# RMSNorm of a matrix product: the order of the last row block's stores, and row block 4 stored in row halves

## The chip, the cores and the metric

One core of a Trainium2 chip. The metric is the device time of one execution in microseconds (us), the median of several. The time of an execution is a little longer than the span of its profile (220.8 against 219.0 us in the profiled run of before); the span runs from the first to the last instruction only.

## The reference

```python
def reference(a, b, gamma, eps):            # a, b: 2048 x 2048 fp32, gamma: 2048
    x = np.matmul(a, b)
    rms = np.sqrt(np.mean(x ** 2, axis=-1, keepdims=True) + eps)
    return (gamma * x / rms).astype(np.float32)
```

## The kernel before

The 2048 rows are 16 row blocks of 128. The product is computed in groups of two row blocks by seven half-size products in place of eight, in 16-bit floats; a group takes two halves `j`, each of which fills 512 columns in each half of the matrix's width. A row block's result sits in two fp32 tiles `x` of 128x1024; it is scaled in place by gamma and the inverse rms, and SyncE stores it. The tiles rotate through a few slots, so a later group writes where an earlier block was.

The store, and the hook that calls it during the following group:

```python
    def store(mb, order=(0, 1)):
        for h in order:
            nc.sync.dma_start(out=rows(mb, h * HALF, (h + 1) * HALF), in_=x_half.pop((mb, h)))
    # ... (hooks of the first half of a group; nxt = 2 * g + 2)
                hook(3, scale, 2 * g - 2)
                hook(4, apply, nxt + 1)
                hook(4, store, 2 * g - 2)
    # ... (hooks of the second half of a group)
            if g + 2 < NG:
                hook(0, load_after, g, nxt + 2)      # 1 MB of input, issued by GpSimd,
                # ...                                # once x_chunk(2 * g + 1, 1) is there
                    hook(0, load_block, nxt + 3)     # 1 MB more
```

The start of a half of a group. `x22` of the group that computes blocks 8 and 9 lies in the slot of block 4's second tile, so ScalarE's copy (L597, after the change L602) has to wait until that tile's store has landed:

```python
        x11, x12, x21, x22 = (x_chunk(ra, c1), x_chunk(ra, c2), x_chunk(rb, c1), x_chunk(rb, c2))
        # ...
        product(g, j, *one)
        nc.scalar.copy(out=c, in_=one[1])            # L597; c is x22
        last_squares()
        at_hook(1)
        product(g, j, *two)
        # ... six more products
```

The end of the last group (`rb` is row block 15, `xb` its left tile, `right` a tile with its right half):

```python
        r_b = inverse_rms(half_sq[:, 1:2], part)
        nc.vector.tensor_scalar_mul(out=xb[:, 0:CH], in0=xb[:, 0:CH], scalar1=r_b)
        nc.sync.dma_start(out=rows(rb, 0, CH), in_=xb[:, 0:CH])               # L809, 256 KB
        by_r(right[:, 0:CH], r_b)                                             # ScalarE
        for bank, col in zip(half, halves):
            scaled_gamma(right[:, CH:][:, col], bank, r_b, gam[3][:, col])    # VectorE
        nc.sync.dma_start(out=rows(rb, HALF, N), in_=right)                   # L813, 512 KB
        by_r(xb[:, CH:], r_b)                                                 # ScalarE
        nc.scalar.dma_start(out=rows(rb, CH, HALF), in_=xb[:, CH:])           # L815, 256 KB
```

Of the kernel before, what the change touches and what calls it, by code (L numbers as in the profile page):

```python
# [17 lines left out]
def kernel(  # L18
# [13 lines left out]
    nc = tc.nc  # L32
    P = 128
# [6 lines left out]
    CH = 512  # L40
    NCH = N // CH
    HALF = N // 2
    HB = 4
# [48 lines left out]
    for h, queue in enumerate((nc.sync, nc.scalar)):  # L92
        queue.dma_start(out=a0f[:, 2 * h:2 * h + 2, :],
                        in_=a[2 * h * P:(2 * h + 2) * P, 0:W2].rearrange("(r p) k -> p r k", p=P))
# [201 lines left out]
    x_half = {}  # L296
# [16 lines left out]
    def x_tile(mb, h):  # L313


        if (mb, h) not in x_half:
            n = n_x[0]
            n_x[0] += 1
            if n < 8:
                slot = n  # L320
            else:
                g = n // 4
                slot = ((0, 4, 1, 5), (0, 1, 4, 5))[g // 2 % 2 == 0][n % 4] + 2 * (g % 2)
            x_half[mb, h] = x_slot[slot]
        return x_half[mb, h]
# [29 lines left out]
    def inverse_rms(last, partial):  # L355
        return inverse(root(last, partial))

    def rows(mb, lo, hi):
        return out[mb * P:(mb + 1) * P, lo:hi]
# [12 lines left out]
                op0=ALU.mult, op1=ALU.mult)  # L372

    def store(mb, order=(0, 1)):
        for h in order:
            nc.sync.dma_start(out=rows(mb, h * HALF, (h + 1) * HALF), in_=x_half.pop((mb, h)))

    def finish(mb, order=(0, 1)):
        for h in order:
            scale(mb, (h,))  # L380
            store(mb, (h,))
# [252 lines left out]
    def hooks_of(g, j):  # L634
# [13 lines left out]
        if j == 0:  # L648
            if g == G0:
# [13 lines left out]
                hook(2, scale, 1, (0,))  # L663
                hook(4, apply, nxt + 1)
                hook(4, store, 1, (0,))
                hook(7, late.insert, 0, (r2, None))
            else:
# [13 lines left out]
                hook(3, row_factor, nxt + 1)  # L681
                hook(4, apply, nxt + 1)
                hook(4, store, 2 * g - 2)
        else:
            if g == G0:
# [19 lines left out]
    def last_group():  # L705
# [3 lines left out]
        ra, rb = 2 * g, 2 * g + 1  # L709
        x11, x12, x21, x22 = ([x_chunk(mb, 2 * j + c) for j in range(2)]  # L710
                              for mb in (ra, rb) for c in range(2))
        xa, xb = x_tile(ra, 0), x_tile(rb, 0)
# [24 lines left out]
        def by_r(x, r):  # L737
            nc.scalar.activation(out=x, in_=x, func=ACTF.Copy, scale=r)  # L738
# [68 lines left out]
        r_b = inverse_rms(half_sq[:, 1:2], part)  # L807
        nc.vector.tensor_scalar_mul(out=xb[:, 0:CH], in0=xb[:, 0:CH], scalar1=r_b)
        nc.sync.dma_start(out=rows(rb, 0, CH), in_=xb[:, 0:CH])  # L809
        by_r(right[:, 0:CH], r_b)  # L810
        for bank, col in zip(half, halves):
            scaled_gamma(right[:, CH:][:, col], bank, r_b, gam[3][:, col])
        nc.sync.dma_start(out=rows(rb, HALF, N), in_=right)  # L813
        by_r(xb[:, CH:], r_b)
        nc.scalar.dma_start(out=rows(rb, CH, HALF), in_=xb[:, CH:])  # L815

    for g in range(G0, NG - 1):
        for j in range(2):
            group_half(g, j, hooks_of(g, j))
    last_group()  # L820

# [33 lines left out]
```

## Time and profile before

| | before |
|---|---|
| median of 3 runs | 220.94 us (220.91 to 221.03) |
| span of the profile | 219.0 us |
| TensorE busy | 95% |
| last matmul's end to the end of the span | 7.0 us |
| last store's issue to its landing | 3.5 us |

The first four lines say that TensorE bounds the kernel up to its last matmul, and that 7 us follow in which it does nothing. A change that touches no matmul can gain only in those 7 us. It can lose anywhere, if it makes TensorE wait.

### The profile page before, as it was taken

Reading aid. Unit: us, or ns where it says so; the run is one execution under the profiler, and the core shown is the slowest. Engines: PE = TensorE matmul, PEld = TensorE weight load, DVE = VectorE, ACT = ScalarE, POOL = GpSimd, SP = SyncE. Lnnn points to the kernel's source line nnn. Section 1 sums busy time; section 2 is a strip of 40 time slices with the busy share of each in tenths; the row PEclk is TensorE's granted clock in tenths of the full one; section 3 lists DMA queues with packets and bytes.
Section 4 is the critical chain, followed back from the end, with each engine's and each line's share of the span. In section 5 each row is a group of like instructions: output and inputs, shape, how many; then the busy total and the mean of one; then the engine's idle time right before and its main releaser. Section 6 shows DMA issues by size and latency. Waiting matters only on the chain.

```text
span 219.0 us, 3023 instructions
## 1 busy us (share of the span) xinstructions
PE 208.8 (95%) x1012; PEld 98.4 (45%) x1032; DVE 165.9 (76%) x326; ACT 127.0 (58%) x263; POOL 36.2 (17%) x75
## 2 busy tenths in 40 slices
PE   7999999999999999999999999999999999999970
PEld 3544544444455444444444444444444444444440
DVE  1228799999899998988794649856794759787781
ACT  2110002920599898788646996289747996334471
POOL 7644433433020002100200002000200000000040
PEclk9999999999999999999999999999999999999996
DMA  7999999999939698939899049955799349145045
GB/s 152 175 202 206 204 206 209 210 208 224 414 91 332 232 278 214 379 153 263 213 294 381 19 87 272 355 233 96 174 291 396 57 89 365 69 178 208 1 179 206
DMA packets 36864, 46.60 MB, mean 213 GB/s; under 512 B 22256, under 2 KB 26352, under 8 KB 35568
## 3 DMA queue, kind: packets, MB, share of 16 engines
q0 software_dynamic: 10608, 23.86, 44.3%
q1 hardware_dynamic: 25824, 22.02, 33.4%
q10 hardware_dynamic: 416, 0.52, 0.7%
q8 instruction: 8, 0.13, 0.2%
q14 instruction: 8, 0.07, 0.1%
HBM read 34.60 MB, written 16.78 MB: 235 GB/s over the span
## 4 chain that ended last, share of the span: by engine, by line
PE 91%; DMA 3%; issue 1%; ACT 1%; POOL 1%; DVE 0%; ACTq 0%; POOLq 0%
PE acc L285 71%; PE acc L388 16%; DMA early<-in_a_dram 3%; PE tbank L419 2%; PE tbank L168 2%; PE acc L799 1%; POOL b L102 0%; PE tbank L185 0%; PE acc L185 0%; ACT x L738 0%; DVE head_at L173 0%; ACT sq L802 0%; ACT rms L352 0%; POOL t_left masks.py:199 0%; POOL t_left masks.py:197 0%
## 5 line engine op out<-in xcount | busy, mean ns | idle before, releaser
L285 PE MATMUL acc<-b,s 128*128 128x512 bf16 x397 | 92.7, 379 | 0.7
L285 PEld LDWEIGHTS <-s 128*128 128x128 f16 (+1 forms) x512 | 50.0, 98 | 59.6 <-DVE s L260 0.2
L388 PE MATMUL acc<-b,head_at 128*128 128x512 bf16 x171 | 42.2, 379 | 0.4 <-DMA b<-in_b_dram 0.3
L303 ACT ACTIVATE sq<-x 128x512 bf16<-128x512 f32 x53 | 33.4, 630 | 6.9 <-DVE x L731 3.0
L370 DVE SCALAR_TENSOR_TENSOR x<-x,r,gamma_sb 128x1024 f32<-128x1024 f32 x28 | 34.9, 1281 | 0.7
L219 ACT ACTIVATE sq<-a 128x1024 bf16<-128x1024 f32 x24 | 25.3, 1053 | 2.0 <-DMA a<-in_a_dram 1.4
L388 PEld LDWEIGHTS <-head_at 128*128 128x128 bf16 x176 | 16.9, 98 | 19.5 <-issue 0.7
L242 ACT ACTIVATE head_at<-a,s 128x2048 f16<-128x2048 f32 x10 | 20.0, 1998 | 3.4 <-DVE s L229 3.3
L102 POOL DMA_DIRECT2D b<-in_b_dram x32 | 17.2, 540 | 20.4 <-DMA b<-in_b_dram 14.1
L430 ACT COPY x<-acc 128x512 f32<-128x512 f32 x5 | 2.9, 582 | 24.6 <-PE acc L388 24.6
L285 PEld LDWEIGHTS <-head_at 128*128 128x128 f16 (+1 forms) x112 | 11.0, 98 | 13.2
L285 PEld LDWEIGHTS <-at_even 128*128 128x128 f16 x96 | 9.4, 98 | 11.3
L285 PE MATMUL acc<-early,head_at 128*128 128x512 bf16 x63 | 14.4, 379 | 0.1
L285 PE MATMUL acc<-early,s 128*128 128x512 bf16 x56 | 14.2, 379 | 0.0
L260 DVE TENSOR_TENSOR s<-head_at 128x1024 f16<-128x1024 f16 (+5 forms) x22 | 13.4, 636 | 0.1
L615 DVE TENSOR_TENSOR x<-x,x 128x512 f32<-128x512 f32 x9 | 6.2, 692 | 8.8 <-ACT x L613 8.3
L127 POOL COPY pace<-x 128x1 f32<-128x1 f32 x4 | 1.7, 413 | 66.3 <-DVE x L624 65.0
L597 ACT COPY x<-acc 128x512 f32<-128x512 f32 x9 | 5.2, 573 | 11.5 <-PE acc L285 7.7
L285 PE MATMUL acc<-t_left,s 128*128 128x512 bf16 x47 | 11.3, 379 | 0.1
L783 POOL TENSOR_SCALAR x<-x,r 128x512 f32<-128x512 f32 x1 | 2.7, 2653 | 51.2 <-DVE r L346 51.2
L276 DVE TENSOR_TENSOR b<-b 128x1024 bf16<-128x1024 bf16 x16 | 10.8, 686 | 0.2
L173 DVE COPY head_at<-tbank 128x1024 bf16<-128x1024 bf16 x7 | 4.8, 692 | 8.0 <-PE tbank L168 7.9
(113 smaller groups left out, 239.3 us busy)
## 6 DMA issues: line engine op xcount, KB each, us to landing
out_dram<-x SPq DMA_DIRECT2D x29, 512.0 KB, 3.7
a<-in_a_dram POOLq DMA_DIRECT2D x10, 1024.0 KB, 8.6
b<-in_b_dram POOLq DMA_DIRECT2D x32, 256.0 KB, 9.9
a<-in_a_dram POOLq DMA_DIRECT2D x4, 512.0 KB, 9.8
early<-in_a_dram POOLq DMA_DIRECT2D x7, 256.0 KB, 10.0
gamma_sb<-in_gamma_dram POOLq DMA_DIRECT2D x2, 512.0 KB, 8.3
out_dram<-x SPq DMA_DIRECT2D x3, 256.0 KB, 2.6
out_dram<-a SPq DMA_DIRECT2D x1, 512.0 KB, 3.3
```

Of the source, the lines that this page charges most:

```text
L102: nc.gpsimd.dma_start(out=raw[j][kp][:, t, :], in_=b[lo:lo + P, j * HALF:(j + 1) * HALF])
L173: nc.vector.tensor_copy(out=head_at[:, 2 * kp:2 * kp + 2, :, :], in_=view)
L219: nc.scalar.activation(out=junk, in_=a32[mb][:, h * HALF:(h + 1) * HALF], func=ACTF.Square, scale=2.0 ** -8, accum_out=n2[:, h:h + 1])
L242: nc.scalar.activation(out=a16[mb], in_=a32.pop(mb), func=ACTF.Copy, scale=factor.pop(mb))
L260: nc.vector.tensor_tensor(out=sum_of(g, s)[:, lo:hi, :], in0=x[:, lo:hi, :], in1=y[:, lo:hi, :], op=op)
L276: nc.vector.tensor_tensor(out=flat[:, 1:3, :], in0=flat[:, 1:3, :], in1=flat[:, 0::3, :], op=ALU.add)
L285: nc.tensor.matmul(bank, lhsT[:, kp, :], rhs, start=(start and kp == 0), stop=(kp == KP - 1), skip_group_check=not start)
L303: nc.scalar.activation(out=sq[:, 0:CH], in_=src, func=ACTF.Square, scale=inv_sqrt_n, accum_out=msq[mb][:, c:c + 1])
L370: nc.vector.scalar_tensor_tensor(out=x, in0=x, scalar=inverse_of[mb], in1=gamma_sb[:, h * HALF:(h + 1) * HALF], op0=ALU.mult, op1=ALU.mult)
L388: nc.tensor.matmul(bank, head_at[:, kt, r, :], head_rhs(c, kt), start=(kt == 0), stop=(kt == KT - 1))
L597: nc.scalar.copy(out=c, in_=one[1])
L615: nc.vector.tensor_tensor(out=t, in0=t, in1=x12, op=ALU.add)
```

## The change

The intent: the last 1 MB of output should go to memory without a hole, from one queue, and its last store should be the one behind which the fewest closing waits stand. ScalarE scales `xb`'s second chunk ahead of `right`'s first. Row block 4 is cut in row halves, two transfers more, by which the transfers' semaphores rotate two further.

```diff
     def store(mb, order=(0, 1)):
+        step = P // 2 if mb == HB else P
         for h in order:
-            nc.sync.dma_start(out=rows(mb, h * HALF, (h + 1) * HALF), in_=x_half.pop((mb, h)))
+            x = x_half.pop((mb, h))
+            for lo in range(0, P, step):
+                nc.sync.dma_start(
+                    out=out[mb * P + lo:mb * P + lo + step, h * HALF:(h + 1) * HALF],
+                    in_=x[lo:lo + step, :])
@@
         nc.sync.dma_start(out=rows(rb, 0, CH), in_=xb[:, 0:CH])
+        by_r(xb[:, CH:], r_b)
+        nc.sync.dma_start(out=rows(rb, CH, HALF), in_=xb[:, CH:])
         by_r(right[:, 0:CH], r_b)
         for bank, col in zip(half, halves):
             scaled_gamma(right[:, CH:][:, col], bank, r_b, gam[3][:, col])
         nc.sync.dma_start(out=rows(rb, HALF, N), in_=right)
-        by_r(xb[:, CH:], r_b)
-        nc.scalar.dma_start(out=rows(rb, CH, HALF), in_=xb[:, CH:])
```

All lines of the kernel after are five further down than those of before: L597 is L602, L376 (the store) is L379.

## The prediction

> **What bounds the kernel now.** I read the page first, then the chain of work that ended last in order of time, then the timeline, the DMA windows and SyncE's waits over the last six microseconds.
>
> ```profile
> span 219.0 us, 3023 instructions
> PE 208.8 (95%) x1012; PEld 98.4 (45%) x1032; DVE 165.9 (76%) x326; ACT 127.0 (58%) x263; POOL 36.2 (17%) x75
> ```
>
> TensorE is busy 95% of the span. The chain, read in order of time, leaves TensorE only at the very end:
>
> ```profile
> 210.21 1.76 PE acc L799 x16
> ...
> 212.05 0.48 ACT sq L802 x2
> ...
> 212.89 0.17 DVE r L346
> ...
> 213.08 0.03 ACT a L738
> 213.11 0.60 issue
> 213.71 0.70 ACT x L738
> ```
>
> Columns are start, duration, what. TensorE's last matmul ends at 211.97. The chain view stops at 214.41, with ScalarE's last scaling, yet the span lasts to 219.0. The missing 4.6 us are a store, its landing and the program's closing waits. Nothing in the change touches a matmul, so a gain can only come from the 219.0 - 211.97 = 7.0 us after the last one, and mostly from those 4.6. The timeline of that stretch (start, duration, engine, line, tile; SPq and ACTq are the sequencers that issue transfers):
>
> ```profile
> 213.08 0.72 ACT L738 ACTIVATE a<-a,r 128x512 f32<-128x512 f32 x1 [0.23 <-DVE r L346]
> 213.09 0.49 DVE L808 TENSOR_SCALAR x<-x,r 128x512 f32<-128x512 f32 x1
> 213.49 0.87 DVE L734 SCALAR_TENSOR_TENSOR a<-acc,r,gamma_sb 128x256 f32<-128x256 f32 x2
> 213.60 0.33 SPq L809 DMA_DIRECT2D out_dram<-x  x1
> 213.71 0.70 ACT L738 ACTIVATE x<-x,r 128x512 f32<-128x512 f32 x1
> 214.42 0.33 SPq L813 DMA_DIRECT2D out_dram<-a  x1
> 214.45 0.36 ACTq L815 DMA_DIRECT2D out_dram<-x  x1
> ```
>
> The reader is to see that the first 256 KB store (L809) leaves at 213.60, and the remaining 768 KB only at 214.42 and 214.45, together. In between, a finished chunk (`right`, done on ScalarE at 213.80) waits for its other half. The windows below show what the 16 DMA engines do (the last two columns are their busy share and GB/s):
>
> ```profile
> 214.50:214.75 0.25, 0.00 (x0) 0.00 (x0) 0.00 (x0) 0.00 (x0) 0.00 (x0) 1.00 0.99 377
> 214.75:215.00 0.25, 0.00 (x0) 0.00 (x0) 0.00 (x0) 0.00 (x0) 0.00 (x0) 0.84 1.01 385
> 215.00:215.25 0.25, 0.00 (x0) 0.00 (x0) 0.00 (x0) 0.00 (x0) 0.00 (x0) 0.50 0.66 205
> ...
> 217.00:217.25 0.25, 0.00 (x0) 0.00 (x0) 0.00 (x0) 0.00 (x0) 0.00 (x0) 0.50 0.89 320
> 217.25:217.50 0.25, 0.00 (x0) 0.00 (x0) 0.00 (x0) 0.00 (x0) 0.00 (x0) 0.50 0.16 49
> ```
>
> They are full from 214.45, sag to 0.66 around 215.2, are full again, and stop at about 217.4. The sag is the hole between L809's packets and those of the two late stores; in the trace's packets it is about 0.17 us per engine (L809's end near 215.15, the next start near 215.3). The end then is:
>
> ```profile
> L850 SPq EVENT_SEMAPHORE  x4: 28/28/28, 217.9 to 218.1; - x4
> L850 SPq DRAIN  x2: 7/7/7, 218.2 to 218.2; - x2
> ```
>
> These are SyncE's instructions of the closing line between 217.7 and 218.3. The last transfer, L815 on ScalarE's queue, lands 3.5 us after its issue (landing column of its line), at 217.90. Only then do four waits follow at 217.92, 217.98, 218.04 and 218.10, one each 0.06 us, then two drains at 218.17 and 218.23, and 0.8 us of barrier to 219.0. SyncE goes through its transfer semaphores in a fixed order, two to an instruction.
>
> [...] both queues are in flight from 215.7 to 217.3 and the rate stays at 352 to 434 GB/s, as with one queue alone (377 and 385 above). [...] L813's first packet comes 0.85 us after its issue, L815's, issued 0.03 us later, 1.23 us after. [...] Here the last packet ends at 217.41 and the landing is at 217.90, 0.49 us. [...]
>
> **The change, part by part.**
>
> (1) *ScalarE's order.* Two 128x512 scalings swap: second chunk `xb[:, 512:]` first, `right[:, 0:512]` second. Both inputs are ready by 212.2, so both orders run 213.08 to 213.80 and 213.71 to 214.41. Cost 0. The order of instructions on TensorE, VectorE and GpSimd is otherwise the same, by comparison of the two programs.
>
> (2) *The stores.* The second chunk's 256 KB can now leave SyncE when its queue is free and ScalarE is done: L809 issues 213.60 + 0.33 = 213.93, ScalarE is done at 213.80, so about 214.0. The last store, 512 KB of `right`, needs both ScalarE at 214.41 (before: VectorE at 214.36) and goes at about 214.45; SyncE, done with the one ahead at 214.35, is in time. So the last issue does not move, but what is behind it shrinks from 768 to 512 KB. Packet time per engine, from the trace: 8 packets of 2 KB at 88 ns = 0.70 for a 256 KB store, 8 of 4 KB at 170 ns = 1.36 for 512 KB. Sum 0.70 + 0.70 + 1.36 = 2.76, in both kernels. Before: 214.45 + 2.76 + hole 0.17 = 217.38 (seen: 217.41 for the last engine). After: L816's packets are there at 214.0 + 0.85 = 214.85, before L814's end at 215.15; the last store's at 214.45 + 0.85 = 215.30, before L816's end at 215.85. No hole: 214.45 + 2.76 = 217.21, say 217.24 for the last engine. Gain 0.17 us.
>
> (3) *Row block 4 in row halves.* Four 256 KB stores take the place of two of 512 KB, around 106 us: two more issues of 0.33 to 0.39 us on SyncE, where the next transpose waits until 124.29. No cost. But the transfers take eight semaphores in rotation, and two more transfers turn it by two. Comparing the waits of the two programs, the transfer that lands last was on number 4 (L815) and is now on number 7, the last of the eight. Without part 3 the new last store would be on number 5. Counting from the closing waits above, three of the waits that stood behind the last landing are passed while the transfer still runs: 3 x 0.06 = 0.18 us gain, of which 0.12 needs the row halves. I take this to be their purpose.
>
> Sum: 0.17 + 0.18 = 0.35 us. 220.94 - 0.35 = 220.59, so I say 220.6.
>
> **The rivals.**
>
> *A: only the closing waits gain.* If one queue with three stores in a row leaves small gaps of its own at the seams, the 0.17 is lost: 220.94 - 0.18 = 220.76. Against it: L782, L787 and L788 followed one another on SyncE's queue at a share of 0.93 or more.
>
> *B: SyncE becomes the bound of the tail.* The second issue could hold the sequencer longer than 0.33 us; after a transpose, issues took 0.95 to 1.17 us (100.2 and 106.5). Then the last store leaves near 215.1, its packets start near 216.0, and a new hole of 0.15 us eats the gain: about 220.75 with the closing waits, up to 221.0 if worse. Against it: no transpose is near, L782 to L813 all took 0.33. The last store has 0.55 us of slack (215.30 against 215.85).
>
> *C: the row halves disturb the middle.* The later rotation and two more issues could hold a slot of x that a later block rewrites, and TensorE would stand: plus 0.1 to 0.5 us. Against it: block 4's tiles are rewritten only by the group that starts after 120 us, and a store lands 3.7 us after its issue.
>
> *D: nothing is seen.* The fetch of instructions through the DMA engines shows on single engines (one straggler held L788's last packets to 214.31); such a straggler in the last store costs 0.1 to 0.3 us and would hide the gain.
>
> **Range and chances.** Main line 220.6 with weight of some 65%; A and B put 220.75, C and D 220.8 to 221.2; a better overlap than I count, 220.4. The runs of before spread 0.12 us. So 220.38 to 220.90 for 8 in 10. Two per cent is 4.4 us, as long as the whole tail from the last issue to the end: chance of faster 0.01, slower 0.01, same 0.98.
>
> **What would show it.** Right: the last three stores' issues at about 213.6, 214.0 and 214.45 after r, all on SyncE; no sag of the DMA share between 214.5 and 217.1; last landing about 0.17 us earlier relative to r; one wait and two drains behind it in place of four and two; the last matmul still at 212.0. Wrong in (2): a sag that has only moved, or the last issue later than 214.6. Wrong in (3): as many waits behind the landing as before. The whole would be wrong if the last matmul moved by more than 0.1 us, or if the time before and after were taken on chips that differ by more than the gain.

## The result, and the profile after

| | before | after |
|---|---|---|
| median (6 runs of each, same chip) | 220.99 us | 222.35 us |
| range | 220.86 to 221.85 | 222.03 to 223.5 |
| ratio of after to before, 95% interval | | 1.0058 (1.0032 to 1.0083) |

A ratio is the mean time of one kernel's fast runs over that of the other's of the same rounds, so it isn't quite the ratio of the medians. The change is a loss of about 1.3 us, within the 2% that counts as the same, and outside the predicted range.

The kernel's profile after comes from its slowest run (223.5 us), which overstates the loss. Its page begins:

```profile
span 221.7 us, 3045 instructions
PE 210.6 (95%) x1032; PEld 98.3 (44%) x1032; DVE 165.9 (75%) x326; ACT 126.9 (57%) x263; POOL 36.2 (16%) x75
```

The span is 2.7 us longer. (PE shows 20 instructions more because the trace of before lacks some matmul records; the weight loads, 1032 in both, are equal.) I split the 2.7 us at two marks. The last matmul starts at 214.13 where it started at 211.68: 2.45 us. From the end of the last reciprocal, called r from here on, to the end it takes 6.23 where it took 5.94: 0.29 us. So most of the loss lies where nothing was expected, ahead of the tail. The 2.45 us are two things. TensorE's weight loads, counted off one by one in both traces, are 1.15 us later by 40 us already, where the inputs came later: that is the start of the kernel, and as much as this run lies above the median (223.5 against 222.35). They stay 1.15 us late to 120 us, and are 2.44 late from 142 us on: the 1.3 us between are the loss in question.

**The middle.** TensorE's waits in the kernel after (what it waited for, us in total, times, longest):

```profile
PE acc L147 <- DVE pace L137: 1.4, 1, 1.4
PE acc L285 <- ACT x L602: 1.1, 1, 1.1
```

These are the two longest. The first is the start of the kernel and is as long in before. The second is new. In the timeline it is one place, the matmuls that take a bank (an accumulator that TensorE writes) again (in the square brackets the idle time ahead of them and who ended it):

```profile
134.79 1.46 PE L285 MATMUL acc<-early,at_even 128*128 128x512 bf16 x6 [1.13 <-ACT x L602]
```

The chain of waits of the kernel after says whence it comes (start, duration, what):

```profile
109.19 1.30 DVE x L370
110.49 0.14 SPq L379
...
110.68 9.35 DMA out_dram<-x
...
120.12 0.04 ACT x L602
```

VectorE's scaling is followed by SyncE's issue of a store, by 9.35 us in which the store is under way, and by ScalarE's copy, behind which ScalarE's further work ran late, down to the same copy of the next half of a group (at 134.18, before at 131.06). It is this later copy's bank that TensorE waited for from 133.66. Here is the same copy in the timeline of before:

```profile
117.01 0.59 ACT L597 COPY x<-acc 128x512 f32<-128x512 f32 x1 [3.84 <-PE acc L285]
```

and of after:

```profile
120.12 0.58 ACT L602 COPY x<-acc 128x512 f32<-128x512 f32 x1 [5.80 <-DMA out_dram<-x]
```

Before, TensorE's product released it; after, a DMA did. The store is that of block 4's second tile. What SyncE issued there (the store's line, durations in ns, first and last start), before:

```profile
L376 SPq DMA_DIRECT2D out_dram<-x x4: 332/421/1165, 106.5 to 110.2; - x4
DMA to landing us min/median/max: 3.7/9.0/11.8
```

and after:

```profile
L379 SPq DMA_DIRECT2D out_dram<-x x6: 558/684/1196, 107.9 to 112.0; - x6
```

Two issues more, and each of them longer, 0.68 in place of 0.42 at the median. Beside these stores GpSimd issues the 2 MB input load of blocks 10 and 11, at 107.69 in before and 109.15 in after, 1.2 us after the first store's issue in both. In before the second tile's store is issued at 107.72, with the load; in after its two halves go at 109.85 and 110.68, behind it. What that does to a store is in the DMA windows (start and end; then the busy time of PE, PEld, DVE, ACT and POOL; granted clock, DMA share, GB/s; a packet counts whole in the window where it starts, so that the share can pass 1), before:

```profile
108.00:109.00 1.00, 1.00 (x6) 0.45 (x5) 1.00 (x2) 0.01 (x1) 0.74 (x2) 1.00 1.13 374
```

and after, one microsecond on the same footing:

```profile
109.46:110.46 1.00, 1.00 (x7) 0.44 (x5) 1.00 (x2) 0.01 (x1) 0.74 (x2) 1.00 1.11 207
```

The engines are as full, and move 207 GB/s in place of 374. The trace's packets show two reasons. A packet of the first 64-row store takes 345 ns, one of a whole store 160. And once the load runs, the trace counts one 8 KB packet of it (309 ns) to one 4 KB packet of the stores (159 ns), so the stores get 64 packets, 256 KB, per 2.0 us: 131 GB/s. The low rate alone is no mark of the row halves, though. Before has it too, two microseconds later, when the second tile's whole rows meet the start of the load (4 KB packets of 305 ns at the median):

```profile
110.00:111.00 1.00, 1.00 (x6) 0.41 (x5) 1.00 (x3) 0.87 (x2) 0.00 (x0) 1.00 1.10 213
```

The sum, on TensorE's own clock. TensorE was 1.15 us later than before already when it released the copy ahead (L613 at 111.25, L608 at 110.10 before). That is the start of the kernel again; at this mark the profiles of kernels with block 4 whole are 0.0 to 0.3 us late, those with block 4 cut 0.3 to 1.5, one profile each, and what makes it is not known. The second tile lands at 120.02 in place of 115.59, 4.43 later, of which 4.43 - 1.15 = 3.28 remains on TensorE's clock. The copy had 117.01 - 115.59 = 1.42 us to spare. With 0.10 from landing to copy, the copy is 3.28 - 1.42 + 0.10 = 1.96 us later. The later copy, and with it the bank, is late by as much; TensorE stands 1.13 us for it, so some 0.8 us were to spare there. (The slack of 1.42 us is that of one run: in the profiles of other kernels with block 4 whole this tile lands 0.55 to 2.5 us ahead of the copy.) From the early copy L613 to this copy it is 8.87 us in after and 6.91 in before, a distance that doesn't contain the start of the kernel; I use it below, as copy to copy, as the mark of the loss.

**The tail.** The lines that answer to the prediction's timeline:

```profile
215.33 0.16 DVE L346 RECIPROCAL r<-rms 128x1 f32<-128x1 f32 x1 [0.50 <-ACT rms L352]
...
216.04 0.33 SPq L814 DMA_DIRECT2D out_dram<-x  x1
216.47 0.38 SPq L816 DMA_DIRECT2D out_dram<-x  x1
216.95 0.39 SPq L820 DMA_DIRECT2D out_dram<-a  x1
```

With r at 215.49 the issues are at r + 0.55, + 0.98 and + 1.46; the prediction's 213.6, 214.0 and 214.45 with r at 213.05 are + 0.55, + 0.95 and + 1.40. And the closing line, behind the last landing at 220.79:

```profile
L855 SPq DRAIN  x2: 7/10/13, 220.9 to 220.9; - x2
L855 SPq EVENT_SEMAPHORE  x1: 28/28/28, 220.8 to 220.8; - x1
```

One wait and two drains, as predicted. (In both traces the closing line passes the eight semaphores of the stores in the order 107, 109, 113 to 118, 0.06 us apart where nothing is awaited; the last landing reports on 115 in before and on 118 in after.) But the last packet ends at r + 4.82 (before r + 4.36) and lands at r + 5.30 (before r + 4.85). The transfer itself became slower, by more than the closing waits gained.

### The profile page after: what moved, and what is told of

Its sections match the earlier page's. It is cut to its first block, busy times and chain, and to the rows that moved or that the text cites. A ratio compares the mean times of both kernels' runs of the same rounds, so it can differ in the third digit from the quotient of the medians.

```text
span 221.7 us, 3045 instructions
## 1 busy us (share of the span) xinstructions
PE 210.6 (95%) x1032; PEld 98.3 (44%) x1032; DVE 165.9 (75%) x326; ACT 126.9 (57%) x263; POOL 36.2 (16%) x75
## 4 chain that ended last, share of the span: by engine, by line
PE 72%; DMA 14%; ACT 6%; POOL 2%; issue 2%; DVE 2%; ACTq 0%; SPq 0%; DVEq 0%; POOLq 0%
PE acc L285 58%; PE acc L393 11%; DMA early<-in_a_dram 5%; DMA b<-in_b_dram 4%; DMA out_dram<-x 4%; ACT sq L219 2%; ACT head_at L242 2%; POOL b L102 1%; PE tbank L424 1%; PE acc L804 1%; PE tbank L168 1%; POOL early L106 1%; ACT sq L303 1%; DVE x L370 1%; PE acc L185 0%
## 5 line engine op out<-in xcount | busy, mean ns | idle before, releaser
L393 PE MATMUL acc<-b,head_at 128*128 128x512 bf16 x176 | 43.4, 380 | 0.3 <-DMA b<-in_b_dram 0.3
L602 ACT COPY x<-acc 128x512 f32<-128x512 f32 x9 | 5.1, 572 | 13.6 <-DMA out_dram<-x 9.8
L285 PE MATMUL acc<-early,at_even 128*128 128x512 bf16 x48 | 10.8, 379 | 1.1 <-ACT x L602 1.1
L788 POOL TENSOR_SCALAR x<-x,r 128x512 f32<-128x512 f32 x1 | 2.7, 2655 | 51.0 <-DVE r L346 51.0
```

Source lines behind the costliest of these rows:

```text
L285: nc.tensor.matmul(bank, lhsT[:, kp, :], rhs, start=(start and kp == 0), stop=(kp == KP - 1), skip_group_check=not start)
L393: nc.tensor.matmul(bank, head_at[:, kt, r, :], head_rhs(c, kt), start=(kt == 0), stop=(kt == KT - 1))
```

## The experiments

All kernels but `tail_far`, which is wrong on purpose, gave correct results, and all executions quoted are fast ones unless a line says otherwise (a kernel run once has no state). All medians and ratios are against runs of before on the same chip in the same rounds. The expectations name theories by a letter, with what each holds written out beside it. In words, four questions are open: which part of the change loses the time; whether the row halves lose by their slow packets or by the two issues more; whether the second tile and the load are what matters; and why the tail's transfer is slow.

### Which part: tail_only and rows_only

`tail_only` has the new tail, with block 4 in whole tiles:

```diff
-        step = P // 2 if mb == HB else P
+        step = P
```

> The tail's new order and single queue alone; row block 4 stored whole. Theory R (the row halves of block 4 carry the loss): 0.2 to 0.35 us faster than before, about 220.7, and TensorE has no wait near 134. Theory T (the tail itself got slower, as the one profile after suggests: 6.4 us from the last reciprocal to the end against 6.1): 0.2 to 0.4 us slower than before, about 221.3.

`rows_only` has the row halves, with the tail as in before:

```diff
-        by_r(xb[:, CH:], r_b)
-        nc.sync.dma_start(out=rows(rb, CH, HALF), in_=xb[:, CH:])
         by_r(right[:, 0:CH], r_b)
         # ...
         nc.sync.dma_start(out=rows(rb, HALF, N), in_=right)
+        by_r(xb[:, CH:], r_b)
+        nc.scalar.dma_start(out=rows(rb, CH, HALF), in_=xb[:, CH:])
```

> The row halves of block 4 alone, the tail as before. Theory R: slower by 1.3 to 1.6 us (the whole loss and the tail's gain on top), a TensorE wait of about 1.1 us on the copy into the second tile of block 4, whose store lands about 3 us later than before against its issue time. Theory T: within 0.3 us of before.

| | median | before beside it | ratio, 95% interval | copy to copy |
|---|---|---|---|---|
| tail_only | 221.30 | 221.09 | 1.0011 (0.9976 to 1.0046) | 6.91 |
| rows_only | 222.42 | 221.09 | 1.0067 (1.0028 to 1.0105) | 9.45 |

The row halves alone lose all of it, about 1.3 to 1.5 us, and show the late copy; the tail alone is not told from before by its times. Its profile still has something to tell: r to end 6.07, landing at r + 5.04, where before has 5.94 and 4.85.

### Slow packets or more issues: cols4, rows_even_odd, cut_first

A 64-row store touches partitions 0 to 63 or 64 to 127. The packets of the first one took 345 ns, those of a whole tile 160; what makes them slow the trace doesn't show. The three kernels keep two further issues, and none has a store of 64 neighbouring partitions.

`cols4` cuts block 4 by columns, all 128 partitions in each piece:

```diff
-        step = P // 2 if mb == HB else P
+        step = CH if mb == HB else HALF
-            for lo in range(0, P, step):
+            for lo in range(0, HALF, step):       # out=rows(mb, h*HALF+lo, ...), in_=x[:, lo:lo+step]
```

> The whole change, but block 4's four stores are cut by columns (128 partitions x 512) in place of rows (64 x 1024): the same number of transfers, issues and semaphores, the same bytes. Theory P (64 neighbouring partitions run at half rate, packets of 330 to 360 ns in place of 160): no loss, about 220.6 to 220.8, the store of the second tile lands near where it did before, under 9 us after the first store's issue. Theory N (two more issues and packets' overhead hold the queue): the loss stays, about 222.2.

`rows_even_odd` takes even rows in one piece and odd rows in the other:

```diff
-        step = P // 2 if mb == HB else P
+        step = 2 if mb == HB else 1
-                    in_=x[lo:lo + step, :])
+                    in_=x[lo::step, :])           # out=out[mb*P+lo:(mb+1)*P:step, ...]
```

> The whole change, but each 64-row store takes every other row (even rows, then odd rows) in place of 64 neighbours: same number of transfers, same 4 KB packets, 64 partitions each. Theory P (the partitions' place decides the rate): first packets take about 160 to 170 ns each, no loss, about 220.6 to 220.8. If it is that only 64 partitions take part, or the number of transfers: packets of 330 ns or more, about 222.2.

`cut_first`, with before's tail, leaves the second tile whole and cuts the first into three by columns:

```diff
+            cuts = (0, 768, 896, HALF) if (mb, h) == (HB, 0) else (0, HALF)
+            for lo, hi in zip(cuts, cuts[1:]):    # out=rows(mb, h*HALF+lo, h*HALF+hi), in_=x[:, lo:hi]
```

> The tail as before; block 4's second tile stored whole, its first tile cut by columns into 768 + 128 + 128, so that only the two further issues stand ahead of the second tile's store. Theory I (what counts is when the second tile's store is issued against the load that starts near 110; two issues more on SyncE put it off by about 0.9 us): it is issued near 108.6 in place of 107.72 (before's time scale), lands near 118 in place of 115.6, the copy on ScalarE waits for it and TensorE waits 1 us or more near 134; time about 222.2. Theory C (only a store that is itself cut lands late): lands under 116, no wait, about 221.0.

| | median | before beside it | ratio, 95% interval | second tile: last issue | issue to landing | copy to copy |
|---|---|---|---|---|---|---|
| before | | | | 107.72 | 7.87 | 6.91 |
| after | 222.35 | 220.99 | 1.0058 (1.0032 to 1.0083) | 109.21 | 9.35 | 8.87 |
| rows_only | 222.42 | 221.09 | 1.0067 (1.0028 to 1.0105) | 109.17 | 9.08 | 9.45 |
| cols4 | 222.45 | 221.09 | 1.0053 (1.0020 to 1.0086) | 108.64 | 9.44 | 9.16 |
| rows_even_odd | 222.92 | 221.09 | 1.0070 (1.0030 to 1.0110) | 108.98 | 8.87 | 9.59 |
| cut_first | 222.74 | 221.07 | 1.0061 (1.0031 to 1.0091) | 108.87 | 9.76 | 9.33 |

(The issue times are shifted so that SyncE's fourth transpose starts where it does in before.) The even and odd rows moved at 181 ns a packet, near the 160 of a whole tile, and the columns go from all 128 partitions; both lose as much as the row halves. So the slow packets of 64 neighbouring partitions are not the cause. `cut_first` goes furthest: the second tile is one ordinary 512 KB store, and it is late because two issues more stand ahead of it. Its copy in the timeline:

```profile
119.98 0.58 ACT L602 COPY x<-acc 128x512 f32<-128x512 f32 x1 [6.27 <-DMA out_dram<-x]
```

So about one microsecond of issue time, spent on stores ahead of it and beside the load, is enough to make the second tile late.

### Is it the second tile and the load: rows_swapped, rows_late, load_later

`rows_swapped` is the kernel after, with block 4's second tile stored first:

```diff
-                hook(4, store, 2 * g - 2)
+                hook(4, store, 2 * g - 2, (1, 0) if 2 * g - 2 == HB else (0, 1))
```

> The whole change, row halves of block 4 and all, but its second tile (which the next group's first copy overwrites) is stored ahead of its first. Theory L: the second tile lands by about 114.6 (before's time scale), before the copy needs it at 117.0; the copy on ScalarE waits for TensorE and not for a transfer; time about 221.0 to 221.2. If the loss comes from elsewhere (the issue time on SyncE, the load arriving late), 222.2.

`rows_late` is the kernel after, with block 12 cut in row halves in place of block 4:

```diff
-        step = P // 2 if mb == HB else P
+        step = P // 2 if mb == MB - 4 else P
```

> The whole change, but the four row-half stores are those of block 12 (stored after 180 us, when no input is being loaded) in place of block 4's. Theory L (cutting a store costs only because the input load that starts about 110 us overtakes the later pieces, and a copy waits for block 4's second tile): no TensorE wait near 134, time that of the tail alone or 0.1 us under it, about 221.0 to 221.2. If cutting a store costs wherever it stands, 222.2. The packets also tell the rate of 64 neighbouring partitions without a load beside: 330 to 345 ns if it is the partitions, 160 if it was the load.

`load_later` is `rows_only` with the load put off until after the stores:

```diff
-                hook(0, load_after, g, nxt + 2)   # and load_block
+                hook(3 if g == G0 + 1 else 0, load_after, g, nxt + 2)
-        wait_for(... x_chunk(2 * g + 1, 1)[:, 0:1])
+        wait_for(... x_chunk(2 * g + 1, 3 if g == G0 + 1 else 1)[:, 0:1])
```

> rows_only (row halves of block 4, tail as before), but the input load of blocks 10 and 11 is held back by a later tile, so that it is issued near 111 in place of 107.7. Theory L: the second tile's last piece lands by about 113.5, the copy waits for TensorE alone, the 1.1 to 1.3 us wait near 134 is gone; time about 221.0 to 221.3. If the pieces are slow of themselves, the landing stays near 118 and the time at 222.4.

| | median | before beside it | ratio, 95% interval | issue to landing | copy to copy |
|---|---|---|---|---|---|
| rows_swapped | 221.37 | 220.96 | 1.0013 (0.9996 to 1.0031) | 7.03 | 6.91 |
| rows_late | 221.49 | 220.96 | 1.0017 (0.9999 to 1.0035) | 6.95 | 6.91 |
| load_later | 223.01 | 221.07 | 1.0061 (1.0015 to 1.0107) | 4.64 | 6.91 |

`rows_swapped` has the same four row halves in the same place, and the loss in the middle is gone:

```profile
118.48 0.58 ACT L602 COPY x<-acc 128x512 f32<-128x512 f32 x1 [3.84 <-PE acc L285]
```

The releaser is TensorE again, and the idle time is to the hundredth that of before. `rows_late` confirms it from the other side: halves where no tile is awaited cost TensorE nothing, although they run as slowly. Its DMA windows, with no load beside it:

```profile
195.50:195.75 0.25, 0.25 (x3) 0.12 (x2) 0.25 (x1) 0.00 (x0) 0.00 (x0) 1.00 0.99 213
```

and before at that place:

```profile
195.00:195.25 0.25, 0.25 (x3) 0.13 (x2) 0.25 (x2) 0.00 (x0) 0.00 (x0) 1.00 1.00 410
```

Something of a loss is left in these two, 0.3 and 0.4 us by the ratios with intervals that reach 1, and both times (221.37 and 221.49) lie above what was expected. Both have the new tail; but in its profile r to the end is 0.05 us longer than in before for `rows_swapped` (5.99) and 0.27 for `rows_late` (6.21), so the tail isn't shown to be all of it. The engines read as full in both windows, at half the bytes. This is where a busy share misleads.

`load_later` hit in the place and missed in the time (221.0 to 221.3 was expected; the median of its fast runs is 222.26, that of all four is in the table). Without the load beside it the second tile landed 4.64 us after its issue, and the copy waited for TensorE, as expected. But the load was then too late for the next group: ScalarE waited 4.1 us for its input, TensorE 3.3, and nothing was won. (Its profile is that of a slow execution, 226.25 us, so the waits' lengths are of that run, and only who released what carries the argument. Its three fast runs are 222.07, 222.26 and 223.76.) So the load can't simply move.

### Why the tail's transfer is slow: tail_two_rings, tail_far, old_order_one_queue, old_tail_turned, old_tail_late

In `tail_only` the rate in the tail falls in two stretches, near r + 2.4 to 2.8 and r + 3.0 to 3.6: a 2 KB packet takes 105 to 121 ns in place of 86, and a 4 KB packet 205 to 258 in place of 162. Its DMA windows (r is at 213.29):

```profile
215.69:216.09 0.40, 0.00 (x0) 0.00 (x0) 0.00 (x0) 0.00 (x0) 0.00 (x0) 0.70 0.99 328
216.09:216.49 0.40, 0.00 (x0) 0.00 (x0) 0.00 (x0) 0.00 (x0) 0.00 (x0) 0.50 1.20 328
216.49:216.89 0.40, 0.00 (x0) 0.00 (x0) 0.00 (x0) 0.00 (x0) 0.00 (x0) 0.50 0.97 338
```

There is no hole, as predicted; the share is full, and the bytes are fewer than the 352 to 434 GB/s of before with two queues in flight.

`tail_two_rings` puts the last store on ScalarE's queue (against `tail_only`):

```diff
-        nc.sync.dma_start(out=rows(rb, HALF, N), in_=right)
+        nc.scalar.dma_start(out=rows(rb, HALF, N), in_=right)
```

> tail_only with the last 512 KB issued from ScalarE's queue in place of SyncE's. In the new tail packets are slow twice, 0.25 to 0.7 us behind each seam between two stores of one queue (2 KB packets 105 to 121 ns in place of 86, 4 KB packets 205 to 258 in place of 162). Theory S (the seam of two stores in one queue): the second slow stretch goes, last landing about 4.85 to 4.9 us after the last reciprocal, against 5.04 in tail_only and 4.85 before. If the slowness is that of the bytes or of where they go: it stays, landing at 5.0 or later.

`tail_far` writes the second chunk to another place in the output, wrong on purpose (the result then fails the comparison, with a relative error that is not a number):

```diff
-        nc.sync.dma_start(out=rows(rb, CH, HALF), in_=xb[:, CH:])
+        nc.sync.dma_start(out=rows(8, CH, HALF), in_=xb[:, CH:])
```

> tail_only, but the 256 KB of the second chunk go to block 8's rows in place of block 15's: a wrong result on purpose. If the slow packets come from writing neighbouring pieces of the same rows shortly after one another, both slow stretches (2.4 to 2.8 and 3.0 to 3.6 us after the last reciprocal) go or shrink, landing about 4.8. If they come from following a store of 2 KB pieces at once with another store, wherever it goes, they stay, landing about 5.05.

`old_order_one_queue` keeps before's order, with the last store on SyncE:

```diff
-        nc.scalar.dma_start(out=rows(rb, CH, HALF), in_=xb[:, CH:])
+        nc.sync.dma_start(out=rows(rb, CH, HALF), in_=xb[:, CH:])
```

> ScalarE's order as before (first chunk of the right half ahead of the second chunk) and the stores in the order of before, but the last 256 KB also on SyncE's queue: no interleaving of two queues. The hole of 0.17 us stays, the last store follows a whole 512 KB store of 4 KB pieces: no slow stretch if only 2 KB stores cause it, last landing 4.85 to 4.9 us after the last reciprocal as before. If one queue as such costs, 5.0 or later.

`old_tail_turned` has before's tail, and turns the semaphores by cutting three tiles of blocks 12 and 13 by columns:

```diff
+            step = CH if mb >= MB - 4 and (mb, h) != (MB - 4, 0) else HALF
+            for lo in range(0, HALF, step):       # out=rows(mb, h*HALF+lo, ...), in_=x[:, lo:lo+step]
```

> The tail as before, block 4 whole; three stores of blocks 12 and 13, after 180 us, are cut in two by columns, so that the rotation turns by three and the store that lands last is on the last of the eight semaphores. From the landing to the end of the span 0.18 us less than before (1.09 us before); the time 0.1 to 0.2 us under before, 220.9 at before's 221.05, though that is inside the spread of single runs.

`old_tail_late` has before's tail, and turns them by block 12 in row halves:

```diff
-        step = P // 2 if mb == HB else P          # of rows_only
+        step = P // 2 if mb == MB - 4 else P
```

> A version meant to keep the one part that worked: tail as before, block 4 whole, the two extra transfers made by cutting block 12's stores into row halves (stored after 190 us, no load beside), so the rotation turns by two and the two last stores stand on the last two of the eight semaphores. No TensorE wait near 134; last landing 4.85 us after the last reciprocal as before, from there to the end 0.95 to 1.0 us in place of 1.09. Time 0.1 us under before, about 220.9, which single runs' spread may hide; clearly over 221.3 would say that cutting late costs too.

All times in this table are us after r, in the profile; a median of one run is only that run.

| | median | before beside it | ratio, 95% interval | last packet | last landing | end | landing to end |
|---|---|---|---|---|---|---|---|
| before | | | | 4.36 | 4.85 | 5.94 | 1.09 |
| after | 222.35 | 220.99 | 1.0058 (1.0032 to 1.0083) | 4.82 | 5.30 | 6.23 | 0.93 |
| tail_only | 221.30 | 221.09 | 1.0011 (0.9976 to 1.0046) | 4.56 | 5.04 | 6.07 | 1.03 |
| tail_two_rings | 221.05 | 220.96 | one run | 4.58 | 5.06 | 6.11 | 1.05 |
| tail_far | 221.36 | 221.07 | one run | 4.72 | 5.21 | 6.26 | 1.05 |
| old_order_one_queue | 221.24 | 221.07 | one run | 4.33 | 5.15 | 6.20 | 1.05 |
| old_tail_turned | 221.13 | 220.96 | 1.0007 (0.9990 to 1.0023) | 4.36 | 4.83 | 5.99 | 1.16 |
| old_tail_late | 220.95 | 221.18 | 0.9984 (0.9968 to 1.0000) | 4.35 | 4.93 | 5.92 | 0.99 |

A second queue changes nothing: the slow stretches stay. In a place seven blocks of 128 rows away they stay too, and this one run landed later still, at r + 5.21. `old_order_one_queue` is the odd one: its last packet ends as early as in before, and lands 0.82 us later where before's took 0.49. In these tails a 256 KB store of 2 KB rows whose packets run alone lands 0.82 to 0.9 us after its last packet, a 512 KB store of 4 KB rows 0.35 to 0.49; where the two interleave at the end, as in before, it is 0.47 to 0.58.

`old_tail_turned` was a design error of mine: with three transfers more the second-to-last store sat on the first semaphore of the fixed order, SyncE waited there and passed the other seven only afterwards, and landing to end grew to 1.16. It gave one thing by the way. Its blocks 12 and 13, cut by columns, ran with 105 to 146 ns per 2 KB packet behind the seams (means of 0.25 us); whole tiles in that place run at 159 to 170 ns per 4 KB packet. So the slow stretches come behind 2 KB rows, away from the tail too. What follows need not have 2 KB rows: the second slow stretch of `tail_only` is in the last store's 4 KB rows. And before itself has such a stretch, which the experiments did not look at: L782 has 2 KB rows, L787 follows it without a hole, and L787's 4 KB packets take some 217 ns on average near r - 1.2. There is none where 4 KB rows are followed by 2 KB rows (`old_order_one_queue`, 85 ns), nor in before behind L809, where the hole lies between. What these runs have in common is a store of 2 KB rows that another store follows without a hole.

`old_tail_late` gained 0.10 us from landing to end against before, with the tail's code unchanged: the closing waits' gain by itself. (It turns by two with before's order, so its last store is on number 6, not 7.) But its landing came 0.08 later, and from r to the end only 0.02 us is left. Its ratio, whose interval touches 1, is thus not explained by the tail, and I draw nothing from it.

In the kernel after there is one thing more. One DMA engine fetched instructions (8 KB) at r - 1.29, which took 1.23 us, and one engine was late with the stores from there on and in a stream without holes never caught up. A landing is complete when all 16 engines have reported: of L793, the store ahead, 15 had by r + 1.72 and the last at 2.68; of the last store, 15 by r + 5.04 and the last at 5.30. Without this engine the landing would be where `tail_only` has it, at 5.04. (That the late engine is the one that fetched is inferred; the trace doesn't number the engines.) In before and `tail_only` the fetch is at r + 0.17 and takes 0.31 us. In all eight kernels of this study with two further issues and a profile of a fast run (after, `rows_only`, `rows_late`, `rows_swapped`, `rows_even_odd`, `cols4`, `cut_first`, `old_tail_late`) it lies between r - 1.13 and r - 1.33, and takes 0.34 to 1.23. With the new tail its length and the landing go together: 1.23 and 5.30 (after), 1.20 and 5.30 (`rows_late`), 0.90 and 5.19 (`cols4`), 0.57 and 5.06 (`rows_swapped`), 0.34 and 5.05 (`rows_even_odd`). Why it lies earlier there, and what makes it long, was not tested.

### Wide rows: tail_wide_rows and wide_turned

If 2 KB rows in succession are what is slow, the left tile should go as one 512 KB store with 4 KB rows, though later. `tail_wide_rows` (against `tail_only`):

```diff
-        nc.sync.dma_start(out=rows(rb, 0, CH), in_=xb[:, 0:CH])
         by_r(xb[:, CH:], r_b)
-        nc.sync.dma_start(out=rows(rb, CH, HALF), in_=xb[:, CH:])
+        nc.sync.dma_start(out=rows(rb, 0, HALF), in_=xb)
```

> tail_only, but the first two chunks leave as one 512 KB store with 4 KB rows once ScalarE is done with the second, and the right half follows on the same queue: two stores, no 2 KB rows, the first packets 0.45 us later. Theory W (runs of 2 KB rows from one store after another are what the memory side takes more slowly): packets of 159 to 175 ns throughout, no slow stretch behind the seam, from last packet to landing about 0.48 us; last landing near 5.0. If following at once is what costs, slow packets of 200 ns and more behind the seam, landing 5.2 or later.

`wide_turned` adds three row-halved stores late, so that the semaphores turn and no tile is awaited:

```diff
-        step = P
+            step = P // 2 if (mb, h) in ((MB - 4, 0), (MB - 4, 1), (MB - 3, 0)) else P
```

> The version that the runs point to: block 15 leaves as two 512 KB stores with 4 KB rows (as in tail_wide_rows), block 4 whole, and three stores of blocks 12 and 13 (after 190 us) in row halves so that the rotation turns by three and the two last stores stand on the last two semaphores. Last landing 4.7 to 4.75 us after the last reciprocal (4.85 before), from there to the end 0.92 to 0.96 (1.09 before), together 0.27 to 0.3 us less; no TensorE wait near 134; time about 220.75 at before's 221.05, ratio near 0.9987.

The DMA windows of `tail_wide_rows` (r is at 213.59, so these are as far after r as those of `tail_only` above):

```profile
215.99:216.39 0.40, 0.00 (x0) 0.00 (x0) 0.00 (x0) 0.00 (x0) 0.00 (x0) 0.99 1.04 430
216.39:216.79 0.40, 0.00 (x0) 0.00 (x0) 0.00 (x0) 0.00 (x0) 0.00 (x0) 0.50 0.97 389
216.79:217.19 0.40, 0.00 (x0) 0.00 (x0) 0.00 (x0) 0.00 (x0) 0.00 (x0) 0.50 1.01 410
```

328, 328 and 338 GB/s have become 430, 389 and 410, at a share near 1 as there. The first issue is later, at r + 0.78 in place of r + 0.55, and the last packet still ends at r + 4.38; the landing is at r + 4.73, 0.31 earlier than in `tail_only` and earlier than the 5.0 expected, the end at r + 5.84. (It also has one store and one seam fewer; that these alone did it was not tested.) `wide_turned` has the landing at r + 4.72 and the end at r + 5.65, landing to end 0.93.

| | median | before beside it | ratio, 95% interval |
|---|---|---|---|
| tail_wide_rows | 221.20 | 221.18 | one run |
| wide_turned | 220.67 | 220.93 | 0.9982 (0.9966 to 0.9998) |

`wide_turned` is 0.26 us below before by the medians, and its interval lies just under 1: the best version of this study, and near the 0.35 us that the prediction hoped for. It is also the lowest of the fifteen versions run here, so that the interval flatters it; what the profile shows is firmer. Its profile's gain from r to the end is 5.94 - 5.65 = 0.29 us.

## Why the prediction was wrong, point by point

- **What bounds the kernel**: right. TensorE is busy 95%, and nothing in the change touches a matmul. The conclusion from it, that the last matmul stays at 212.0, was wrong: a change that touches no matmul still moved one, through a tile that was stored late (1.3 of the 2.45 us that the profile shows; the rest is its start).
- **Step (1), ScalarE's order costs nothing**: right. Issues at r + 0.55, 0.98 and 1.46, predicted 0.55, 0.95 and 1.40; the last matmul's start to r is unchanged (1.37).
- **Step (2), the stream gains 0.17 us**: wrong in sign. The hole closed as computed, but the packet durations that were summed (0.70 + 0.70 + 1.36) came from a tail in which no store followed 2 KB rows without a hole. Landing moved from r + 4.85 to r + 5.04 in `tail_only`, 0.19 later in place of 0.17 earlier, and to r + 5.30 with the late engine. The runs support that 2 KB rows with a store straight behind them are the cause (`tail_wide_rows` removes them and the slow stretches with them). Why this is slow is not settled; moving the second chunk elsewhere and a second queue for the last store did not help.
- **Step (3), closing waits gain 0.18**: right. Landing to end is 0.93 in place of 1.09, 0.16 us, and split nearly as it said: 1.03 in `tail_only`, without the row halves.
- **Step (3), "two more issues of 0.33 to 0.39 us on SyncE ... No cost"**: this is the step that failed. It looked at whether SyncE had time, which it had. It didn't look at what the stores behind those issues would meet. Block 4's four issues took 0.58 to 1.2 us each; the second tile's store then came behind a 2 MB load, landed 9.35 us after its issue, and held ScalarE's copy 1.96 us and TensorE 1.13.
- **Rival C named this mechanism and was dismissed on two numbers.** "Block 4's tiles are rewritten only by the group that starts after 120 us": the copy was at 117.01. "A store lands 3.7 us after its issue": that is the page's median of all 29 such stores and the least of the four issued here, 3.7/9.0/11.8; this very store took 7.87. Both were in the profile of before, and gave a slack of 1.42 us rather than the ten or so that the two numbers leave. How far the landing would move could not be read there; the runs show 3.28 us.
- **Rival A** (only the closing waits gain) came nearest for the tail, though even it was too hopeful. It was set aside on the DMA share of L782, L787 and L788, 0.93 or more; but the share stays full where the packets are slow (0.97 to 1.20 at 328 to 338 GB/s in `tail_only`), and behind L782 they were. The prediction's "352 to 434 GB/s" with both queues in flight leaves out the 320 of its own last full window. **B** did not occur: the issues took 0.33 to 0.39. **D**'s straggler did occur in the profiled run.
- **The range** took the runs' spread as 0.12 us, that of three runs; six runs of before spread 0.99. Even so, the miss (222.35 against 220.90 at most) is no bad luck: in the same rounds the slowest run of before is 221.85, the fastest of after 222.03.
- **The sum**: predicted -0.17 - 0.18. Measured in the medians +1.36. `rows_only` alone has +1.33. `rows_swapped` differs from the change only in the order of block 4's two tiles, and its ratio is 1.0013 in place of 1.0058: the wait for the second tile is about 1.0 us, with intervals of some 0.5 us to either side. The rest, 0.3 to 0.4 us, lies in the tail and the start, and the times don't split it.

## What to carry to other kernels

Before adding an issue to a queue, follow what is behind it to its landing, not to its issue: find who writes that buffer next, read that store's own landing time rather than the column's minimum or median, and take the difference as the slack. If a large load starts nearby, a microsecond of issue time can cost the store behind it far more (here 3.28 us of landing), and the cure is to store first what is needed first (`rows_swapped`), or to place the harmless extra transfers where nobody waits (`wide_turned`). And a full DMA share says nothing about bytes (here 0.99 at 213 GB/s and 1.00 at 410): compare GB/s at the same share before summing packet times from another place.
